# The half-wide chunk of a feed-forward block by seven products: half a slab of the down projection moved ahead of its last block, and the order of ScalarE and VectorE written out by hand

## The chip, the core and the metric

The kernel runs on one core of one Trainium2 chip. The core has TensorE (PE) for matmuls, which reads SBUF and writes PSUM; VectorE (DVE) and ScalarE (ACT) for elementwise work; GpSimd (POOL); and SyncE (SP), which mostly issues transfers. ACT and POOL issue some transfers too. Each engine has its own queue and works through it in order; engines wait for each other by semaphores. The metric is the time of one execution on the device in microseconds (us), and the median of several runs is compared.

## What is computed

Two layers over 256 tokens of width 1024. Each layer has a feed-forward block, a mixer (a gated convolution, a recurrence and a pooling), a cross attention over 256 rows of memory, and a second feed-forward block, each with a residual and a layer norm behind it:

```
def swiglu(x, w_gate, w_up, w_down):
    return (jax.nn.silu(x @ w_gate) * (x @ w_up)) @ w_down

for l in range(DEPTH):
    h = layer_norm(ALPHA * h + 0.5 * swiglu(h, ffn1_gate[l], ffn1_up[l], ffn1_down[l]), ln_g[l, 0], ln_b[l, 0])
    ...
    h = layer_norm(ALPHA * h + mix, ln_g[l, 1], ln_b[l, 1])
    h = layer_norm(ALPHA * h + cross_attn(h, mem, ca_q[l], ca_k[l], ca_v[l], ca_o[l]), ln_g[l, 2], ln_b[l, 2])
    h = layer_norm(ALPHA * h + 0.5 * swiglu(h, ffn2_gate[l], ffn2_up[l], ffn2_down[l]), ln_g[l, 3], ln_b[l, 3])
```

All is float32; the inner width of the feed-forward block is 2816.

## The kernel before

**Halves of a number.** A float32 product is made of three matmuls on rounded parts. `split` (L74) makes the parts: ACT rounds a tile (the cast on L75, `whi` or `ah`), then DVE subtracts the rounded from the whole (L76, `wlo` or `al`, called the rest below). `mm_rows` (L153) multiplies the rounded by the rounded, the rounded by the rest, and the rest by the rounded. Each weight loaded from memory goes through such a split, 1024 columns of 128 partitions at a time.

**Chunks.** A feed-forward block (`ffn`, L420) goes through its inner width in chunks of 512 columns, and a last one of 256, number 5, the half-wide chunk. For each chunk it makes gate and up products, the activation times the up product (called acts), and then multiplies acts by rows of the down matrix into four banks that add up over the block (`both`, L765). Rows of the down matrix come in slabs of two times 128 (`slab`, L741): (3,0) and (3,1) belong to chunk 3, (4,0) and (4,1) to chunk 4, (5,0) to chunk 5. A slab is two splits, an ACT cast and a DVE rest for each.

**By seven products.** Some chunks are made by `by_seven` (L600) with seven products of 2x2 blocks in place of eight: chunks 2 and 4, and chunk 5 in every feed-forward block but the first. `run` (L650) is one block product of 12 matmuls for a bank `o[n]`, `parts_of` (L633) adds two weight blocks on DVE where it is told to (L637) and splits the sum, `taken` (L668) copies a bank to SBUF on ACT (L669), and `put` (L655) adds or subtracts a bank on DVE (L656). In the half-wide chunk the steps of L691 to L696 run in reverse order: first the product for `o[3]`, then the one that adds to `o[0]` and is copied to `f`; then comes the last block, with the weights w00 + w10 added and split for it (L698). Ahead of these, `taken(e, o[0])` (L687) copies the bank that the reversed step writes again.

**Dealing.** The acts have to be turned, so that the inner width lies on the partitions. `turn` (L464) issues four transfers that deal out the gated tile (L469); for the half-wide chunk two are on SP and two on ACT. Its inner function `rest` makes the transposes on DVE (L475) and splits the result into `ah` and `al` (L480). `left` (L700) runs the activation of the second half (L454) and a sum, and `gate_all` (L704) multiplies by the up product (L705) and calls `turn`.

**Order.** The program's text gives priorities; a scheduler puts each engine's instructions in order at build time. `tc.issue_after(x)` ties instructions of the block to come behind `x` on the engine of `x`, and leaves the other engines free. In the half-wide chunk the list `between` names what is put between the blocks: half of slab (3,0) (its `k` = 0), and the dealing of chunk 4's acts. Behind the chunk (L806 to L812) come the transposes and split of chunk 4's acts, tied behind the last rest on DVE; then activation, product and turning of chunk 5's acts in one call; then the other half of slab (3,0) and slab (3,1). Slabs (4,0), (4,1) and (5,0) are loaded on L816 and multiplied in `ending` (L822), for the first 128 tokens and then for the second. `finish` (L323) makes the layer norm of the first 128 tokens while PE works on the second, and PE transposes the result (L196) ahead of its last 12 matmuls of the block where another stage follows.

Of the kernel before, what the change touches and what calls it, by code (L numbers as in the profile page):

```python
# [11 lines left out]
AF = mybir.ActivationFunctionType  # L12
# [48 lines left out]
def model(ctx: ExitStack, tc: tile.TileContext, t: dict, out: bass.AP):  # L61
# [12 lines left out]
    def split(hi, lo, src):  # L74
        nc.scalar.copy(hi, src)  # L75
        lows.append(nc.vector.tensor_tensor(lo, src, hi.bitcast(F32), op=ALU.subtract))  # L76
# [343 lines left out]
    def ffn(l, name, n, pend=None, last=False, early=None):  # L420
        gate, up, down = (t[f"{name}_{x}"][l] for x in ("gate", "up", "down"))
        with tc.tile_pool(name="ffn", bufs=2, reuse_waits="tile") as fp:
# [24 lines left out]
            def ordered(v):  # L447
                return v.rearrange("p (a k j) -> p a k j", a=4, j=32)

            def in_order(o):  # L450
                return o.rearrange("p (a j k) -> p a k j", a=4, j=32)

            def activate(s, i, og):
                nc.scalar.activation(ordered(s[:, i, :]), in_order(og), AF.Silu)  # L454

            def gated(s, i, ou):
                v = ordered(s[:, i, :])
# [6 lines left out]
            def turn(s):  # L464
                n = s.shape[2] // P
                x = fp.tile([P, 4, NT, P], F32, tag="dealt", name="dealt", bufs=1)[:, :, :, 0 : 32 * n]
                for a in range(4):
                    queue = nc.scalar if n < 4 and a % 2 else nc.sync
                    queue.dma_start(x[a * 32 : a * 32 + 32], s[:, :, a * 32 * n : (a + 1) * 32 * n])  # L469

                def rest():
                    ah, al = act_tiles()
                    d = fp.tile([P, NT, 4, P], F32, tag="up", name="square", bufs=1)[:, :, 0:n, :]
                    for i in range(NT):
                        nc.vector.transpose(  # L475
                            d[:, i].rearrange("p k (b r) -> p b k r", b=4),
                            x[:, :, i, :].rearrange("p b (k j) -> p b k j", k=n),
                        )
                    d = d.rearrange("p i k t -> p k i t")
                    split(*(y[:, 0:n].rearrange("p k (i t) -> p k i t", i=NT) for y in (ah, al)), d)  # L480
                    return ah, al

                return rest
# [116 lines left out]
            def by_seven(c0, ncol, bx, between):  # L600
# [54 lines left out]
                def put(o, a, op, b):  # L655
                    nc.vector.tensor_tensor(ordered(o), in_order(a), ordered(b), op=op)  # L656
# [8 lines left out]
                def bank():  # L665
                    return acc((P, CHUNK))[:, 0:ncol]

                def taken(o, bank):  # L668
                    nc.scalar.copy(ordered(o), in_order(bank))  # L669

                def more(to, m, j):
                    for i, x in enumerate(to):
# [11 lines left out]
                run(o[0], bx[1], parts_of(w00, w11), True)  # L684
                if ncol == CHUNK:
                    more(w00, gate, 1)
                taken(e, o[0])  # L687
                between[1]()
                nc.scalar.activation(s[:, 0, :], s[:, 0, :], AF.Silu)
                put(e, o[1], ALU.subtract, e)  # L690
                steps = [  # L691
                    lambda: (run(o[0], bx[2], parts_of(w01), True), taken(f, o[0])),
                    lambda: (o.append(bank()), run(o[3], bx[3], parts_of(w11))),
                ]
                for step in steps if ncol == CHUNK else steps[::-1]:
                    step()  # L696
                put(f, o[1], ALU.subtract, f)
                run(o[0], part_of_x(1, 1), parts_of(w00, None if ncol == CHUNK else w10), True)  # L698

                def left():  # L700
                    activate(s, 1, o[0])
                    put(e, o[3], ALU.add, e)

                    def gate_all():  # L704
                        passed.append(nc.vector.tensor_tensor(s, s, ef, op=ALU.mult))  # L705
                        return turn(s)

                    return gate_all
# [3 lines left out]
            def last_hidden(c0, turn=None):  # L712

                ah, al = act_tiles()
                s = activations()[:, 0, :].rearrange("p (j c) -> p j c", j=2)
                r = fp.tile([P, NT, CHUNK], F32, tag="up", name="up", bufs=1)[:, 0, :].rearrange("p (j c) -> p j c", j=2)
                for m, o in ((gate, s), (up, r)):
                    if turn and m is gate:
                        with tc.issue_after(passed[-1].ins):
# [25 lines left out]


            sevens = (2, 4) if early is not None else (2, 4, 5)
            passed, turn_memory = [], None
            bx = []

            if early is None:
# [23 lines left out]
            for c, (c0, ncol) in enumerate(chunks):  # L775
                if not c:
                    acts.append(first()())
                    ys = [[acc((P, 512), "dn") for _ in range(2)] for _ in range(NT)]
                elif c in sevens:
                    half = []  # L780

                    def deal_last():
                        acts[4] = acts[4]()

                    left = by_seven(
                        c0, ncol, bx,
                        [lambda: both(*todo.pop(0))] * 2 if ncol == CHUNK else
                        [lambda: (half.append(slab(3, 0)), both(3, 0, half[0], (0,))), deal_last],
                    )
                else:  # L790
                    acts.append(hidden(c0)() if ncol == CHUNK else last_hidden(c0, turn_memory))
# [563 lines left out]
```

## Time and profile before

| | |
|---|---|
| median of 3 runs | 1067.07 us (1066.81 to 1068.54) |
| the profiled execution, its own time | 1067.7 us |
| its span, from the first to the last instruction | 1066.0 us |
| granted clock of PE, mean | 0.999 |
| bytes moved | 251.06 MB, mean 236 GB/s |

A row of the order of time reads: start in us from the span's beginning, duration in us, engine, line, operation, the tile written, an arrow, the tiles read, shapes, and xN where N instructions in a row are merged; what stands in brackets is how long the engine sat idle before it, and what ended that. Durations of instructions that follow each other on an engine overlap a little, so the step from one start to the next is what an instruction costs its engine. SPq and ACTq are the sequencers that issue transfers. The three half-wide chunks by seven stand near 495 to 510, 663 to 678 and 1021 to 1036 us of the span; the first is the one quoted.

### The profile page before, as it was taken

Reading aid. Unit: us, or ns where it says so; the run is one execution under the profiler, and the core shown is the slowest. Engines: PE = TensorE matmul, PEld = TensorE weight load, DVE = VectorE, ACT = ScalarE, POOL = GpSimd, SP = SyncE. Lnnn points to the kernel's source line nnn. Section 1 sums busy time; section 2 is a strip of 40 time slices with the busy share of each in tenths; the row PEclk is TensorE's granted clock in tenths of the full one; section 3 lists DMA queues with packets and bytes.
Section 4 is the critical chain, followed back from the end, with each engine's and each line's share of the span. In section 5 each row is a group of like instructions: output and inputs, shape, how many; then the busy total and the mean of one; then the engine's idle time right before and its main releaser. Section 6 shows DMA issues by size and latency. Waiting matters only on the chain.

```text
span 1066.0 us, 16501 instructions
## 1 busy us (share of the span) xinstructions
PE 1053.4 (99%) x6014; PEld 935.8 (88%) x6014; DVE 933.8 (88%) x1246; ACT 661.9 (62%) x909; POOL 90.8 (9%) x122
## 2 busy tenths in 40 slices
PE   9999999999999999999999999999999999999997
PEld 7888888889899888888888888888898998888886
DVE  6998898989988789887998987989899788899887
ACT  6675775677557566655665756666764655675661
POOL 8001001000000001010001001010000000000000
PEclk9999999999999999999999999999999999999999
DMA  9999984754675589978788987866636665799862
GB/s 364 293 317 274 259 276 151 256 169 157 207 277 178 165 282 237 357 188 223 246 295 229 332 248 204 273 221 221 200 119 220 241 236 172 239 291 305 242 188 68
DMA packets 143745, 251.06 MB, mean 236 GB/s; under 512 B 12784, under 2 KB 53520, under 8 KB 143664
## 3 DMA queue, kind: packets, MB, share of 16 engines
q1 hardware_dynamic: 130656, 228.89, 64.4%
q0 software_dynamic: 10800, 19.55, 10.7%
q10 hardware_dynamic: 2208, 1.57, 0.5%
q8 instruction: 47, 0.77, 0.3%
q14 instruction: 34, 0.28, 0.1%
HBM read 234.50 MB, written 1.05 MB: 221 GB/s over the span
## 4 chain that ended last, share of the span: by engine, by line
PE 93%; DVE 4%; issue 1%; ACT 1%; DMA 1%; DVEq 0%; ACTq 0%
PE acc L129 61%; PE dn L129 29%; DVE wlo L76 2%; PE acc L196 1%; DVE raw L637 1%; ACT whi L75 1%; PE dn L1040 0%; DMA lng<-in_ln_g_dram 0%; DMA h<-in_x_dram 0%; PE dn L1114 0%; PE acc L517 0%; DVE halves L656 0%; PE dn L1113 0%; PE dn L1102 0%; PE acc L1182 0%
## 5 line engine op out<-in xcount | busy, mean ns | idle before, releaser
L75 ACT CAST whi<-raw 128x1024 fp32r<-128x1024 f32 (+1 forms) x453 | 457.1, 1042 | 207.8 <-PE dn L129 62.8
L76 DVE TENSOR_TENSOR wlo<-raw,whi 128x1024 fp32r<-128x1024 f32 (+1 forms) x453 | 534.8, 1210 | 54.6 <-ACT whi L75 49.9
L129 PE MATMUL acc<-whi,xT 128*128 128x512 f32 (+1 forms) x1064 | 314.1, 373 | 0.0
L129 PEld LDWEIGHTS acc<-whi,xT 128*128 128x128 f32 x1064 | 199.1, 189 | 27.5 <-ACT both L669 0.9
L129 PE MATMUL acc<-wlo,xT 128*128 128x512 f32 (+1 forms) x532 | 197.9, 372 | 0.0
L129 PE MATMUL dn<-whi,ah 128*128 128x512 f32 x346 | 131.5, 380 | 0.0
L129 PE MATMUL dn<-wlo,ah 128*128 128x512 f32 x346 | 131.1, 379 | 0.0
L129 PE MATMUL dn<-whi,al 128*128 128x512 f32 x346 | 130.8, 379 | 0.0
L129 PE MATMUL acc<-xT,whi 128*128 128x512 f32 x480 | 117.8, 382 | 0.2
L129 PEld LDWEIGHTS acc<-wlo,xT 128*128 128x128 f32 x532 | 100.6, 189 | 13.2
L129 PEld LDWEIGHTS acc<-xT,whi 128*128 128x128 f32 x480 | 86.6, 190 | 10.5 <-ACT whi L75 0.7
L129 PE MATMUL dn<-whi,xT 128*128 128x512 f32 x288 | 87.7, 380 | 0.0
L129 PEld LDWEIGHTS dn<-whi,al 128*128 128x128 f32 x346 | 65.4, 189 | 9.3
L129 PEld LDWEIGHTS dn<-whi,ah 128*128 128x128 f32 x346 | 65.4, 189 | 9.0
L129 PEld LDWEIGHTS dn<-wlo,ah 128*128 128x128 f32 x346 | 65.4, 189 | 8.9
L129 PEld LDWEIGHTS acc<-xT,wlo 128*128 128x128 f32 x480 | 62.9, 191 | 3.2
L129 PE MATMUL acc<-whi,kTh 128*128 128x512 f32 (+1 forms) x176 | 62.0, 352 | 3.2 <-ACT both L669 3.2
L129 PE MATMUL acc<-xT,wlo 128*128 128x256 f32 x480 | 63.2, 275 | 0.0
L129 PE MATMUL acc<-wlo,kTh 128*128 128x512 f32 (+1 forms) x176 | 61.7, 351 | 0.0
L129 PE MATMUL acc<-whi,kTl 128*128 128x512 f32 (+1 forms) x176 | 61.7, 351 | 0.0
L129 PEld LDWEIGHTS dn<-whi,xT 128*128 128x128 f32 x288 | 54.4, 189 | 7.4
L129 PE MATMUL dn<-wlo,xT 128*128 128x512 f32 x144 | 54.6, 379 | 0.0
(245 smaller groups left out, 1291.2 us busy)
## 6 DMA issues: line engine op xcount, KB each, us to landing
raw<-in_ffn_up_dram SPq DMA_DIRECT2D x88, 512.0 KB, 5.4
raw<-in_ffn_down_dram SPq DMA_DIRECT2D x88, 512.0 KB, 5.7
raw<-in_ffn_gate_dram SPq DMA_DIRECT2D x84, 512.0 KB, 5.6
raw<-in_w_in_dram SPq DMA_DIRECT2D x48, 512.0 KB, 4.5
dealt<-sg SPq DMA_DIRECT2D x80, 128.0 KB, 4.8
raw<-in_ffn_up_dram POOLq DMA_DIRECT2D x19, 512.0 KB, 6.1
raw<-in_ffn_gate_dram POOLq DMA_DIRECT2D x16, 512.0 KB, 9.9
raw<-in_ca_k_dram SPq DMA_DIRECT2D x16, 512.0 KB, 5.2
```

Of the source, the lines that this page charges most:

```text
L75: nc.scalar.copy(hi, src)
L76: lows.append(nc.vector.tensor_tensor(lo, src, hi.bitcast(F32), op=ALU.subtract))
L129: nc.tensor.matmul(o, w, x, start=start, stop=stop, skip_group_check=more)
L196: turns.append(nc.tensor.transpose(pt[:, k, :], src[:, (4 * j + k) * P : (4 * j + k + 1) * P], unit))
L637: nc.vector.tensor_tensor(r[i], r[i], plus[i], op=ALU.add)
```

## The change

In the half-wide chunk, and behind it:

- the cast for w00 + w10 is tied behind the copy of L687 on ACT;
- the second half of slab (3,0) moves from behind the chunk to between the copy to `f` and the last block;
- the split of chunk 4's acts (not its transposes) is held back, until the activation of L454 has been issued on ACT and the product of L705 on DVE;
- the transposes and the split of chunk 5's acts move from ahead of slab (3,1) to behind the loads of (4,0) and (4,1);
- the splits of (4,0), (4,1) and (5,0) and of chunk 5's acts are tied behind the last transfer that deals chunk 5's acts (that one is issued on ACT, so the tie holds the casts) and behind the product of L705 (so it holds the rests); the last two also behind the last rest of (4,1).

Chunks of 512 columns keep their order; `activate` and `taken` only return their instruction.

```diff
@@ turn
-                    queue.dma_start(x[a * 32 : a * 32 + 32], s[:, :, a * 32 * n : (a + 1) * 32 * n])
-
-                def rest():
+                    last_deal = queue.dma_start(x[a * 32 : a * 32 + 32], s[:, :, a * 32 * n : (a + 1) * 32 * n])
+
+                deals.append(last_deal)
+
+                def rest(behind=None):
...
-                    split(*(y[:, 0:n].rearrange("p k (i t) -> p k i t", i=NT) for y in (ah, al)), d)
+
+                    def parts():
+                        split(*(y[:, 0:n].rearrange("p k (i t) -> p k i t", i=NT) for y in (ah, al)), d)
+
+                    if behind is None:
+                        parts()
+                    else:
+                        behind.append(parts)
                     return ah, al
@@ by_seven
-                taken(e, o[0])
+                copied = taken(e, o[0])
                 between[1]()
                 nc.scalar.activation(s[:, 0, :], s[:, 0, :], AF.Silu)
                 put(e, o[1], ALU.subtract, e)
-                steps = [
-                    lambda: (run(o[0], bx[2], parts_of(w01), True), taken(f, o[0])),
-                    lambda: (o.append(bank()), run(o[3], bx[3], parts_of(w11))),
-                ]
-                for step in steps if ncol == CHUNK else steps[::-1]:
-                    step()
-                put(f, o[1], ALU.subtract, f)
-                run(o[0], part_of_x(1, 1), parts_of(w00, None if ncol == CHUNK else w10), True)
+                if ncol == CHUNK:
...
+                else:
+                    o.append(bank())
+                    run(o[3], bx[3], parts_of(w11))
+                    run(o[0], bx[2], parts_of(w01), True)
+                    taken(f, o[0])
+                    put(f, o[1], ALU.subtract, f)
+                    with tc.issue_after(copied.ins):
+                        w = parts_of(w00, w10)
+                    between[2]()
+                    run(o[0], part_of_x(1, 1), w, True)
 
                 def left():
-                    activate(s, 1, o[0])
+                    act = activate(s, 1, o[0])
                     put(e, o[3], ALU.add, e)
 
                     def gate_all():
-                        passed.append(nc.vector.tensor_tensor(s, s, ef, op=ALU.mult))
+                        passed.append((act, nc.vector.tensor_tensor(s, s, ef, op=ALU.mult)))
                         return turn(s)
@@ ffn
-                        [lambda: (half.append(slab(3, 0)), both(3, 0, half[0], (0,))), deal_last],
+                        [lambda: (half.append(slab(3, 0)), both(3, 0, half[0], (0,))), deal_last, lambda: both(3, 0, half[0], (1,))],
...
                     if ncol < CHUNK:
+                        held = []
                         with tc.issue_after(lows[-1].ins):
-                            acts[4] = acts[4]()
-                    acts.append(left() if c + 1 in sevens else left()()())
+                            acts[4] = acts[4](held)
+                    acts.append(left() if c + 1 in sevens else left()() if c == 5 else left()()())
                     if ncol < CHUNK:
-                        both(3, 0, half[0], (1,))
+                        with tc.issue_after(passed[-1][0].ins), tc.issue_after(passed[-1][1].ins):
+                            held[0]()
                         both(3, 1)
...
-            end = [slab(4, 0), slab(4, 1), slab(5, 0)]
+            with ExitStack() as behind:
+                if 5 in sevens:
+                    behind.enter_context(tc.issue_after(deals[-1].ins))
+                    behind.enter_context(tc.issue_after(passed[-1][1].ins))
+                end = [slab(4, 0), slab(4, 1)]
+                if 5 in sevens:
+                    behind.enter_context(tc.issue_after(lows[-1].ins))
+                    acts[5] = acts[5]()
+                end.append(slab(5, 0))
```

More of the change, by code (lines that the diff above doesn't have):

```diff
@@ L453, in activate @@
             def activate(s, i, og):
-                nc.scalar.activation(ordered(s[:, i, :]), in_order(og), AF.Silu)
+                return nc.scalar.activation(ordered(s[:, i, :]), in_order(og), AF.Silu)
             def gated(s, i, ou):
@@ L668, in taken @@
                 def taken(o, bank):
-                    nc.scalar.copy(ordered(o), in_order(bank))
+                    return nc.scalar.copy(ordered(o), in_order(bank))
                 def more(to, m, j):
@@ L690, in by_seven @@
                 put(e, o[1], ALU.subtract, e)
[L691 to L698 removed]
+                if ncol == CHUNK:
[4 more added lines that the diff above has]
+                    put(f, o[1], ALU.subtract, f)
+                    run(o[0], part_of_x(1, 1), parts_of(w00), True)
+                else:
+                    o.append(bank())
+                    run(o[3], bx[3], parts_of(w11))
+                    run(o[0], bx[2], parts_of(w01), True)
+                    taken(f, o[0])
+                    put(f, o[1], ALU.subtract, f)
+                    with tc.issue_after(copied.ins):
+                        w = parts_of(w00, w10)
+                    between[2]()
+                    run(o[0], part_of_x(1, 1), w, True)
                 def left():
[L701 removed]
+                    act = activate(s, 1, o[0])
                     put(e, o[3], ALU.add, e)
                     def gate_all():
[L705 removed]
+                        passed.append((act, nc.vector.tensor_tensor(s, s, ef, op=ALU.mult)))
                         return turn(s)
@@ L718, in last_hidden @@
                     if turn and m is gate:
-                        with tc.issue_after(passed[-1].ins):
+                        with tc.issue_after(passed[-1][1].ins):
                             turn(0, 0)
@@ L747, in ffn @@
             sevens = (2, 4) if early is not None else (2, 4, 5)
-            passed, turn_memory = [], None
+            passed, deals, turn_memory = [], [], None
             bx = []
```

## The prediction

> **What bounds the kernel now.** I read the page first, then who waited for whom on TensorE (PE), then the order of time on PE, ScalarE (ACT) and VectorE (DVE) around the half-wide chunk.
>
> ```profile
> PE 1053.4 (99%) x6014; PEld 935.8 (88%) x6014; DVE 933.8 (88%) x1246; ACT 661.9 (62%) x909; POOL 90.8 (9%) x122
> PE 93%; DVE 4%; issue 1%; ACT 1%; DMA 1%; DVEq 0%; ACTq 0%
> PE acc L129 <- ACT both L669: 3.2, 3, 1.1
> ```
>
> The first row is busy time, the second the chain that ended last, the third the one wait of PE that is not at the kernel's start: three times, 1.1 us each, PE waits for the copy on L669. That is the half-wide chunk, once in each of the three feed-forward stages that have it by seven products. PE is busy 1053.4 of 1066.0 us, so no more than some 12 us of gaps can be won anywhere, and here no more than what the next fence shows. It is PE in the first of the three stages (start, duration, what):
>
> ```profile
> 504.91 0.28 PE L129 MATMUL acc<-wlo,kTh 128*128 128x256 f32 x1
> 505.02 0.28 PE L129 MATMUL acc<-whi,kTl 128*128 128x256 f32 x1
> 506.42 0.38 PE L129 MATMUL acc<-whi,kTh 128*128 128x256 f32 x1 [1.13 <-ACT both L669]
> 506.64 0.28 PE L129 MATMUL acc<-wlo,kTh 128*128 128x256 f32 x1
> ...
> 508.08 0.38 PE L129 MATMUL dn<-wlo,ah 128*128 128x512 f32 x1
> 508.30 0.38 PE L129 MATMUL dn<-whi,al 128*128 128x512 f32 x1
> 508.59 0.38 PE L129 MATMUL acc<-whi,xT 128*128 128x256 f32 x1
> ...
> 510.03 0.38 PE L129 MATMUL dn<-whi,ah 128*128 128x512 f32 x1
> ```
>
> A 256-column matmul follows the one before it by 0.11 us (504.91 to 505.02), a 512-column one by 0.216 (508.08 to 508.30). So the gap at 505.02 costs 1.40 - 0.11 = 1.29, the slow step behind it 0.22 - 0.11 = 0.11, the step at 508.30 0.29 - 0.22 = 0.07: **1.47 us in a stage, 4.4 in three**. That is all that the change can win on PE here. Now ACT and DVE:
>
> ```profile
> 505.06 1.04 ACT L75 CAST whi<-raw 128x1024 fp32r<-128x1024 f32 x1 [2.88 <-DVE raw L637]
> 506.01 0.37 ACT L669 COPY both<-acc 128x256 f32<-128x256 f32 x1
> 506.27 1.99 ACT L75 CAST whi<-raw 128x1024 fp32r<-128x1024 f32 x2
> 508.16 0.37 ACT L669 COPY both<-acc 128x256 f32<-128x256 f32 x1
> 508.43 2.00 ACT L75 CAST whi<-raw 128x1024 fp32r<-128x1024 f32 x2
> 510.40 1.04 ACT L75 CAST ah<-square 128x1024 fp32r<-128x1024 f32 x1
> 511.35 0.38 ACT L454 ACTIVATE both<-acc 128x256 f32<-128x256 f32 x1
> 511.63 1.98 ACT L75 CAST whi<-raw 128x1024 fp32r<-128x1024 f32 x2
> 513.58 1.55 ACTq L469 DMA_DIRECT2D dealt<-both  x2
> 515.17 1.99 ACT L75 CAST whi<-raw 128x1024 fp32r<-128x1024 f32 x2 [1.56 <-DVE wlo L76]
> ```
>
> ```profile
> 503.75 1.22 DVE L637 TENSOR_TENSOR raw<-raw 128x1024 f32<-128x1024 f32 x1
> 506.13 1.23 DVE L76 TENSOR_TENSOR wlo<-raw,whi 128x1024 fp32r<-128x1024 f32 x1 [1.17 <-ACT whi L75]
> 507.27 0.42 DVE L656 TENSOR_TENSOR both<-acc,both 128x256 f32<-128x256 f32 x1
> 507.61 1.22 DVE L76 TENSOR_TENSOR wlo<-raw,whi 128x1024 fp32r<-128x1024 f32 x1
> ...
> 509.08 1.29 DVE L475 STREAM_TRANSPOSE square<-dealt 128x512 f32<-128x512 f32 x2
> ...
> 511.73 1.22 DVE L76 TENSOR_TENSOR al<-square,ah 128x1024 fp32r<-128x1024 f32 x1
> 512.86 0.69 DVE L705 TENSOR_TENSOR both<-both 128x512 f32<-128x512 f32 x1
> 513.46 6.90 DVE L76 TENSOR_TENSOR wlo<-raw,whi 128x1024 fp32r<-128x1024 f32 x6
> 520.27 0.77 DVE L475 STREAM_TRANSPOSE square<-dealt 128x256 f32<-128x256 f32 x2
> 520.96 1.18 DVE L76 TENSOR_TENSOR wlo<-raw,whi 128x1024 fp32r<-128x1024 f32 x1
> 522.07 0.68 DVE L76 TENSOR_TENSOR al<-square,ah 128x512 fp32r<-128x512 f32 x1
> ```
>
> ```profile
> 510.00:525.00 15.00, 15.00 (x72) 13.15 (x72) 14.60 (x18) 8.22 (x10) 0.00 (x0) 1.00 0.88 283
> ```
>
> The cause of the gap is plain: at 505.06 ACT casts the last weights (w00 + w10), having stood 2.88 us for their addition on DVE (503.75), and the copy that PE waits for stands behind that cast until 506.01. The last row counts busy time in the 15 us behind it: PE 15.00, no gap, but DVE 14.60, nearly as full. From 506.13 on, DVE hardly stops. So PE and DVE bind together here, and a change that brings PE forward has to bring DVE's chain forward too.
>
> **The change part by part** (times of this first stage).
>
> *The copy ahead of the cast.* The block that fills the copied bank is the 12 matmuls before the 12 that end with 505.02, so its last starts at 505.02 - 12 x 0.111 = 503.69. The second copy started at 508.16, 0.41 behind the last matmul of its block (506.64 + 10 x 0.111 = 507.75); so the first can start at 504.10 and is done at 504.47, before PE's next block wants it at 505.13. The cast stays at 505.06, since its addition ends at 504.97. Gain: 1.29 + 0.11. DVE may also do the subtraction of 507.27 in its idle 1.17 us before 506.13, which frees 0.33 (507.27 to 507.61).
>
> *Half a slab ahead of the last block.* No work is added; 12 matmuls of 512 columns move. PE: block of 12 from 505.13 to 506.47 (12 x 0.111), half slab to 509.06 (12 x 0.216), last block to 510.40. Its second copy could start at 506.36 + 0.41 = 506.77; should two casts go first it still ends by 508.3; the weights' rests are ready at 507.36. Both are hidden behind the half slab, and the 0.07 goes. Without that cover the block would wait for the copy. But the last block now ends at 510.40, where its last matmul stands about 0.4 us later than today's.
>
> *Activation before the cast to ah.* Today the activation waits behind the cast of 510.40 and starts at 511.35. Now it starts at 510.29 + 0.41 = 510.70 and ends at 511.08. DVE's product on L705 needs DVE as well: from 506.13 it has two rests at 1.135 (six rests take 520.27 - 513.46 = 6.81), a subtraction 0.33, two transposes 1.25, another sum 0.33 and the second rest of slab (3,1) 1.135, until 511.46. The product then ends at 512.15 instead of 513.55. The rest al moves behind it; it is wanted only after slab (3,1), so it costs nothing if something else is slower.
>
> *Slabs (4,0), (4,1) behind the dealing.* This is the part that costs. Today the casts of (4,0) stand at 508.43 and those of (4,1) at 511.63, both ahead of the two transfers that ACT issues at 513.58. The change ties them, and so everything that DVE does with them, behind these. The transfers wait for the product (512.15) and take ACT 1.55 us: to 513.73. First cast to 514.78, its rest from 514.82 to 516.04. DVE has only al to do between 512.06 and that point (to 513.28) and stands idle for some 1.6 us. PE comes from the last block with 24 matmuls of slab (3,1), 510.40 + 5.18 = 515.58, and wants that rest with its second matmul, 515.79: 0.3 late. The second rest comes 1.135 later, where PE has 0.65 of work between: 0.5 late. The two of (4,1) come in time, since each half there serves 12 matmuls, 2.6 us. Then transposes (0.69 from start to start, 520.27 to 520.96), a rest 1.135, al 0.60, a rest 1.135 from 519.36: the last starts at 521.79 and ends at 523.0, some 0.65 behind PE's need. **Given back: 0.3 + 0.5 + 0.65 = 1.45.** Nothing in the queues of SP or POOL is moved past these; SP issues loads as buffers come free, so those of the next stage's weights start 1.3 us later (they wait for the first rest of (4,0), 514.68 today, 516.04 then).
>
> [...] Were issuing free for ACT, the casts would start at 512.2, the rests could follow al without a gap, and the stage would keep nearly all of its 1.45.
>
> *Acts of the last chunk behind the rests of (4,1).* The transposes stand today at 520.27 and would stand at 519.36. Their data land in time:
>
> ```profile
> DMA to landing us min/median/max: 2.3/2.8/3.4
> 525.13 0.69 DVE L352 SCALAR_TENSOR_TENSOR h<-h,dn 128x512 f32<-128x512 f32 x1 [0.17 <-PE dn L129]
> 530.11 1.04 PE L196 MATMUL acc<-pdn,h 128*128 128x128 f32 x8
> ```
>
> Issued by 513.0, landed by 516.4 at the slowest. The other two rows are the normalization of the first half: 5.0 us from its last sum to its transposes on PE, with PE full until then. This leaves no slack, so if next-stage rests (one at 520.96 today) come between, PE waits for what they cost. That is bounded from below by nothing and from above by one rest, 1.135, in two of the stages (behind the last one there is no next). I take 0: the rests come later with their loads, and a higher-priority sum goes first.
>
> **The sum.** 1.47 off, 1.45 back in each stage, three stages: 0.0 on the profiled execution, whose span is 1066.0 and whose own time is 1067.7; the median of the runs is 1067.07, 0.6 below. Forecast **1067.1 us**. Unknowns: DVE's order. If the product goes ahead of the second rest of (3,1), the chain starts 0.35 sooner: -0.4 a stage. If a next-stage rest comes ahead of the last ones, +1.1 in each of two stages. So the likeliest case's own range is 1065.6 to 1069.2.
>
> **Rivals.** *The whole stall goes and nothing takes its place.* PE could be given other matmuls at the late rests: those with the cast half alone (c. 1 us earlier than the rest), or the second half of the tokens. For it: the casts come 1.26 us ahead of the rests (505.06, then 506.13 + 1.23), and PE's order is not fixed by hand there. Against it: DVE's chain to 523.0 stays, and the normalization follows it. It gives 2.2 to 4.4 less: 1062.7 to 1064.9, middle 1063.8.
>
> *Slower: DVE's idle time before the held rests decides.* From the point where ACT's casts wait for the transfers, DVE loses 1.6 us; the same rests, plus the next stage's, then stand ahead of the first half's normalization, and PE waits at the transposes of 530.11. Price, in the two stages that have a next one: one rest, 1.135, ahead of the last slab, and a second, half hidden, 0.57, at the transposes: 3.4 in all, 1070.5; from 2.3 (the first alone, 1069.4) to 4.5 (both whole, 1071.6). It decides from the moment when one next-stage rest is put ahead of the last slab's. For it: at 520.96 one stands there today. Against it: its load starts 1.3 us later.
>
> *The change does not do what it says*: the copy is issued first but PE still waits, as its bank is not free. Against: nothing else stands in front of that copy. It would be 0.0 for the copy and some 1.4 us a stage for the held slabs, 1071; I give it 2 in 100, within the slower case.
>
> **How the numbers follow.** Forecast 0.46, full gain 0.25, slower 0.29. About 0.2% (2.1 us) is what a measurement of this kernel tells from no change. Nearly all of the full gain lies beyond it; of the likeliest case about 0.01 each way. Faster 0.25, same 0.46, slower 0.29. The range leaves out the far quarter of the gain (0.06) and the far third of the slower case (0.10): 1063.2 to 1070.9.
>
> **What would show it.** Right: PE's wait for L669 is gone; the activation starts near 510.7 and the product ends near 512.2 on this clock; ACT has no cast of a slab between it and its two transfers; DVE idles 1 to 2 us before the first rest of (4,0); and PE shows new gaps of 0.3 to 0.7 us at slabs (4,0) and (5,0), adding up to some 1.4. Wrong: no gap there (gain), or a gap of a microsecond at the transposes (loss).

## The result, and the profile after

| | median (us) | runs | over before |
|---|---|---|---|
| before | 1067.12 | 8, 1066.67 to 1068.61 | |
| after | 1069.83 | 8, 1069.39 to 1073.36 | 1.0029 [1.0017, 1.0042] |

The change made the kernel slower: by 2.7 us by the medians, and by a ratio of 1.0029 whose interval is clear of 1. That is inside the range, on the side of the slower rival; the likeliest case, no change, did not come true.

The profiled execution of the kernel after took 1073.36 us, the longest of its eight, so stages are compared here more than spans. In this execution the first half-wide chunk stands some 0.5 us later than before, PE having waited longer for its input at the start (1.1 us, and 0.6 before): the last block, forecast from 509.06, starts at 509.58. That is the shift of 0.52 below. In the code after, L678 is the copy of L669, L723 the product of L705, L477 the transposes of L475; L352 is the sum that ends a half of the down projection, and L362, L366, L373, L378 are the four steps of its normalization on DVE.

First the busy time on the page:

```profile
PE 1055.8 (99%) x6014; PEld 936.4 (87%) x6014; DVE 933.4 (87%) x1246; ACT 662.8 (62%) x909; POOL 91.2 (9%) x122
```

Then who waited for whom on PE (in total, times, longest):

```profile
PE acc L196 <- DVE h L378: 3.7, 2, 1.9
PE dn L129 <- DVE wlo L76: 1.3, 2, 1.0
```

The wait for the copy (3.2 us in three stages) is gone. In its place stand two waits of 1.9 us at the transposes of the normalized first half, and one of 1.0 for a rest. The two rows sum to 5.0, 1.8 more than the row that went.

The spans of the two profiled executions lie further apart, 1066.0 and 1071.4 us. PE's rows divide the 5.4 us. The half-wide chunk of the first stage starts 0.5 later. From its first row to the transposes PE takes 1.0 longer (495.95 to 530.11 before, 496.47 to 531.63 after), and 0.8 longer in the second stage (664.06 to 698.16, 665.83 to 700.70). Between the stages 2.4 are lost, an estimated 1.8 of it to the lower clock of the last section. The third stage takes 0.1 longer up to the last matmul, and 0.6 more pass behind that (7.34 and 7.96 us to the end); the cause of these 0.6 was not looked for.

PE in the first stage, in order of time:

```profile
506.99 0.38 PE L129 MATMUL dn<-whi,ah 128*128 128x512 f32 x1
...
509.36 0.38 PE L129 MATMUL dn<-whi,al 128*128 128x512 f32 x1
509.58 0.27 PE L129 MATMUL acc<-whi,xT 128*128 128x256 f32 x1
...
516.12 1.03 PE L129 MATMUL dn<-whi,ah 128*128 128x512 f32 x4
...
521.75 0.38 PE L129 MATMUL dn<-wlo,ah 128*128 128x512 f32 x1
522.25 0.48 PE L129 MATMUL dn<-whi,ah 128*128 128x512 f32 x1
...
529.40 0.38 PE L129 MATMUL dn<-whi,al 128*128 128x512 f32 x1
531.63 1.29 PE L196 MATMUL acc<-pdn,h 128*128 128x128 f32 x8 [1.85 <-DVE h L378]
```

Half slab and last block run without a gap. At 516 PE runs four products with the rounded acts and weights in a row, where it would have waited for a rest. At slab (5,0) one step of 0.50 is left, and then no gap of that size until the transposes, a step of 2.23. Why their data are late stands in ACT's and DVE's order:

```profile
504.51 0.37 ACT L678 COPY both<-acc 128x256 f32<-128x256 f32 x1 [1.51 <-PE acc L129]
505.87 2.94 ACT L75 CAST whi<-raw 128x1024 fp32r<-128x1024 f32 x3 [0.99 <-DVE raw L646]
508.71 0.36 ACT L678 COPY both<-acc 128x256 f32<-128x256 f32 x1
511.12 0.38 ACT L454 ACTIVATE both<-acc 128x256 f32<-128x256 f32 x1 [2.04 <-PE acc L129]
...
512.92 1.57 ACTq L469 DMA_DIRECT2D dealt<-both  x2
514.54 5.78 ACT L75 CAST whi<-raw 128x1024 fp32r<-128x1024 f32 x6 [2.10 <-DVE al L76]
```

```profile
512.21 0.68 DVE L723 TENSOR_TENSOR both<-both 128x512 f32<-128x512 f32 x1
512.81 1.22 DVE L76 TENSOR_TENSOR al<-square,ah 128x1024 fp32r<-128x1024 f32 x1
515.62 4.63 DVE L76 TENSOR_TENSOR wlo<-raw,whi 128x1024 fp32r<-128x1024 f32 x4 [1.59 <-ACT whi L75]
520.17 0.77 DVE L477 STREAM_TRANSPOSE square<-dealt 128x256 f32<-128x256 f32 x2
...
522.23 0.69 DVE L76 TENSOR_TENSOR al<-square,ah 128x512 fp32r<-128x512 f32 x1 [0.19 <-ACT ah L75]
522.84 2.35 DVE L76 TENSOR_TENSOR wlo<-raw,whi 128x1024 fp32r<-128x1024 f32 x2
525.11 0.68 DVE L352 SCALAR_TENSOR_TENSOR h<-h,dn 128x512 f32<-128x512 f32 x1
...
525.71 0.69 DVE L352 SCALAR_TENSOR_TENSOR h<-h,dn 128x512 f32<-128x512 f32 x1
...
526.32 1.22 DVE L76 TENSOR_TENSOR wlo<-raw,whi 128x1024 fp32r<-128x1024 f32 x1
527.46 0.21 DVE L362 TENSOR_SCALAR mv<-st 128x1 f32<-128x1 f32 x1
528.74 0.69 DVE L352 SCALAR_TENSOR_TENSOR h<-h,dn 128x512 f32<-128x512 f32 x1 [1.06 <-PE dn L129]
...
529.35 0.15 DVE L366 TENSOR_SCALAR rs<-mv 128x1 f32<-128x1 f32 x1
```

Behind its activation ACT rounds ah, and then makes no cast until 514.54: it waits for the product and issues the two transfers. DVE idles 1.59 and 0.19 us. Eight rests of weights (and two of acts, `al`) follow the product before the mean (L362) is made: six of the slabs and two of the next stage. The first of these two ends the pair of 522.84; the second, at 526.32, has fallen into the normalization, between the two sums and the mean. Behind the mean the second half's sum (528.74) stands ahead of `rs`, so that `rs` comes 1.89 us behind the mean. In the kernel before it came 1.52 behind, with nothing between:

```profile
525.86 0.21 DVE L362 TENSOR_SCALAR mv<-st 128x1 f32<-128x1 f32 x1
527.38 0.15 DVE L366 TENSOR_SCALAR rs<-mv 128x1 f32<-128x1 f32 x1 [1.31 <-ACT kTh L365]
```

On the clock of the kernel before, the second sum stands at 525.19 (525.71 less 0.52), where it stood at 525.13, and the mean at 526.94, where it stood at 525.86. So up to the sums DVE is no later than before; it only fails to follow PE's lead. What makes this stage slower than before comes behind the sums: a rest that before stood ahead of them, and the sum ahead of `rs`.

In the third stage, which no next one follows, another step is displaced: a sum on L339 that waits for PE stands ahead of the held rests, on DVE, and PE then waits for the first of these:

```profile
1046.53 0.69 DVE L339 SCALAR_TENSOR_TENSOR h<-h,dn 128x512 f32<-128x512 f32 x1 [2.60 <-PE dn L129]
1047.13 3.49 DVE L76 TENSOR_TENSOR wlo<-raw,whi 128x1024 fp32r<-128x1024 f32 x3
```

### The profile page after: what moved, and what is told of

Read it like the earlier page. It is cut to its first block, busy times and chain, and to the rows that moved or that the text cites. A ratio compares the mean times of both kernels' runs of the same rounds, so it can differ in the third digit from the quotient of the medians.

```text
span 1071.4 us, 16492 instructions
## 1 busy us (share of the span) xinstructions
PE 1055.8 (99%) x6014; PEld 936.4 (87%) x6014; DVE 933.4 (87%) x1246; ACT 662.8 (62%) x909; POOL 91.2 (9%) x122
## 3 DMA queue, kind: packets, MB, share of 16 engines
q10 hardware_dynamic: 2208, 1.57, 0.5%
## 4 chain that ended last, share of the span: by engine, by line
PE 86%; DVE 5%; issue 3%; DMA 3%; ACT 1%; POOL 0%; ACTq 0%; DVEq 0%; SPq 0%; POOLq 0%
PE acc L129 58%; PE dn L129 25%; DVE wlo L76 2%; DMA raw<-in_ffn_gate_dram 2%; PE acc L196 1%; ACT whi L75 1%; DVE raw L646 1%; DMA raw<-in_w_out_dram 0%; PE dn L1068 0%; DMA h<-in_x_dram 0%; PE dn L1142 0%; PE acc L526 0%; DMA dealt<-both 0%; DVE h L378 0%; DVE yr L1221 0%
```

## The experiments

All times are medians, each with its ratio to runs of the kernel before on the same chip, and its interval. "Idle" is DVE's idle time in the first stage from the product to the mean, without the waits for PE; "L196" is PE's wait at the transposes, in total.

| kernel | us | ratio | idle | L196 |
|---|---|---|---|---|
| after | 1069.83 | 1.0029 [1.0017, 1.0042] | 1.78 | 3.7 |
| copy_first | 1065.90 | 0.9987 [0.9978, 0.9996] | 0 | 0 |
| half_back | 1071.09 | 1.0037 [1.0024, 1.0050] | 1.61 | 3.3 |
| slabs_free | 1064.15 | 0.9972 [0.9962, 0.9982] | 0 | 0 |
| casts_free | 1063.38 | 0.9966 [0.9953, 0.9978] | 0 | 0 |
| split_early | 1072.61 | 1.0054 [1.0041, 1.0068] | 2.98 | 3.7 |
| next_later | 1068.62 | 1.0015 [1.0006, 1.0024] | 1.66 | 2.2 |
| free_next | 1064.81 | 0.9977 [0.9968, 0.9986] | 0 | 0.5 |
| flips_first | 1064.35 | 0.9974 [0.9965, 0.9982] | 0 | 0 |
| behind_act | 1072.51 | 1.0040 [1.0026, 1.0054] | 1.80 | 3.7 |
| casts_flips | 1064.93 | 0.9973 [0.9963, 0.9984] | 0.40 | 0 |
| sp_deal | 1067.68 | 1.0006 [0.9997, 1.0015] | 0.94 | 3.3 |
| sp_next | 1066.59 | 0.9993 [0.9984, 1.0002] | 0.69 | 2.3 |

### The copy alone (copy_first)

```diff
@@ the kernel before
-                taken(e, o[0])
+                copied = taken(e, o[0])
...
-                run(o[0], part_of_x(1, 1), parts_of(w00, None if ncol == CHUNK else w10), True)
+                with nullcontext() if ncol == CHUNK else tc.issue_after(copied.ins):
+                    w = parts_of(w00, None if ncol == CHUNK else w10)
+                run(o[0], part_of_x(1, 1), w, True)
```

> The kernel before with one edit of the change: the cast of w00 + w10 tied behind the copy on ACT. If PE alone binds behind the half-wide chunk, all of its stall goes, 1.4 us in each of three stages: about 1063. If DVE's chain binds there with it, as the working of the prediction has it, only what DVE wins goes on to the end (one subtraction, 0.33 us, done in its idle time): 0.3 to 0.6 us a stage, about 1065.8, and the transposes of the first half's normalization wait for DVE. If the copy itself were the cause of the slower time, this would be slower than before.

By the medians it is 1.2 us faster than before. That is the time that the expectation gives for DVE's chain, but not by its mechanism: the transposes do not wait for DVE at all (L196 is 0). The copy's own wait is gone, and the next copy's takes its place, at the last block. Who waited:

```profile
PE acc L129 <- ACT both L669: 2.2, 3, 0.8
```

And PE at that place:

```profile
507.07 0.38 PE L129 MATMUL dn<-whi,ah 128*128 128x512 f32 x1
508.19 0.38 PE L129 MATMUL acc<-whi,xT 128*128 128x256 f32 x1 [0.74 <-ACT both L669]
```

So of 3.2 us waited, 2.2 come back one block later, which is what the half slab is there to cover.

### The half slab put back (half_back)

```diff
@@ the kernel after
-                        [lambda: (half.append(slab(3, 0)), both(3, 0, half[0], (0,))), deal_last, lambda: both(3, 0, half[0], (1,))],
+                        [lambda: (half.append(slab(3, 0)), both(3, 0, half[0], (0,))), deal_last],
...
-                    between[2]()
...
                             held[0]()
+                        both(3, 0, half[0], (1,))
                         both(3, 1)
```

> The changed kernel with the second half of slab (3,0) put back behind the chunk; everything else stays. If the later last block (its last matmul 0.4 us later, and all the chain of activation, product and dealing behind it) is the loss, some 0.5 to 1 us a stage comes back: 1067 to 1068. If the held slabs are the loss, the chain only starts somewhat sooner and PE meets a new short wait at the last block: within 0.7 of the changed kernel, 1069 to 1070.

The wait at the last block is back, as in the experiment before:

```profile
PE acc L196 <- DVE h L378: 3.3, 2, 1.6
PE acc L129 <- ACT both L678: 2.2, 3, 0.7
```

PE waits 0.7 in each stage there, and 0.2 less at each transposes. The time, 1071.09, lies above both ranges of the expectation and 1.3 us above after's, but the two intervals overlap. So the later last block is not the loss; that the half slab hides the copy is shown by the row, and its worth in this kernel is not fixed.

### The held slabs let go (slabs_free, casts_free)

```diff
@@ slabs_free
-                if 5 in sevens:
-                    behind.enter_context(tc.issue_after(deals[-1].ins))
-                    behind.enter_context(tc.issue_after(passed[-1][1].ins))
                 end = [slab(4, 0), slab(4, 1)]
+                if 5 in sevens:
+                    behind.enter_context(tc.issue_after(deals[-1].ins))
+                    behind.enter_context(tc.issue_after(passed[-1][1].ins))
```

In casts_free only the first of the two ties, that behind the transfer, is moved.

> The changed kernel without one tie: slabs (4,0) and (4,1) are not held behind the dealing and the product (acts of chunk 5 and slab (5,0) still are). If the 1.6 us that DVE idles behind the held casts are the loss, the idle time goes, the transposes no longer wait 1.9 us for the normalization in the first two stages and the gap of 1.3 us in the third stage goes: 1065 to 1066.5, faster than before. If the moved half slab is the loss, it stays near 1069.5.

> The changed kernel with the casts of slabs (4,0) and (4,1) no longer behind the dealing on ACT; their rests stay behind the product on DVE. If the loss is the time that ACT stands in the transfers (product, 1.55 us of issuing, then the first cast), it is gone and the time is within 0.7 of the version with the slabs wholly free, 1064.2: 1063.5 to 1065. If the rests held on DVE carry it, it stays above 1068.

These are the two best versions; both came out somewhat faster than was expected of them (casts_free by 0.1 us). casts_free differs from the kernel after in one tie, that of the casts of (4,0) and (4,1) behind ACT's second transfer, and that is worth 6.4 us: 1069.83 to 1063.38. ACT and DVE in its first stage:

```profile
507.62 2.96 ACT L75 CAST whi<-raw 128x1024 fp32r<-128x1024 f32 x3
510.49 0.37 ACT L454 ACTIVATE both<-acc 128x256 f32<-128x256 f32 x1
```

```profile
510.89 0.69 DVE L723 TENSOR_TENSOR both<-both 128x512 f32<-128x512 f32 x1
511.50 1.22 DVE L76 TENSOR_TENSOR wlo<-raw,whi 128x1024 fp32r<-128x1024 f32 x1
...
524.34 0.21 DVE L362 TENSOR_SCALAR mv<-st 128x1 f32<-128x1 f32 x1
525.86 0.15 DVE L366 TENSOR_SCALAR rs<-mv 128x1 f32<-128x1 f32 x1 [1.31 <-ACT kTh L365]
```

Three casts are done while ACT waits for the last block (it stood idle 2.04 us there in the kernel after), a rest is ready at once behind the product, and `rs` follows the mean by 1.52 again. From the activation to the mean it is 13.85 us (510.49 to 524.34) against 16.34 (511.12 to 527.46). Of the 2.49, 1.78 is DVE's idle time and 0.69 the product, which comes 1.09 behind the activation and not 0.40.

### More idle time (split_early)

```diff
@@ the kernel after
-                            acts[4] = acts[4](held)
+                            acts[4] = acts[4]()
...
-                        with tc.issue_after(passed[-1][0].ins), tc.issue_after(passed[-1][1].ins):
-                            held[0]()
```

> The changed kernel with the split of chunk 4's acts as before, not held behind the activation and the product. DVE then has nothing at all between the product and the held rests, but product, transfers and casts stand 1 us later, as the cast to ah is ahead of the activation again. If the chain from the last block to the held casts sets the time, this is slower than the changed kernel by 0.3 to 0.9 in each stage: 1070.5 to 1072.5. If holding that split is itself harmful, it is faster than 1069.5.

Here the rest al of chunk 4 goes ahead of the product, and DVE has nothing left for the time of the transfers: it idles 2.98 us and not 1.78, and the time is 2.8 us above after's. The two intervals just touch (1.0042 and 1.0041), so that holding that split back helps is likely and not more.

### The next stage's rests moved (next_later, free_next)

Both tie the splits of the next stage's first weights behind the mean of the first half on DVE; next_later in the kernel after, free_next in slabs_free.

```diff
+                if i == 0:
+                    means.append(mean)
...
-                wg = load(gate, 0, NK, 0, CHUNK, fine=pend is None)
-                wu = load(up, 0, NK, 0, CHUNK) if pend is not None else None
+                with tc.issue_after(means[-1].ins) if l and name == "ffn1" else nullcontext():
+                    wg = load(gate, 0, NK, 0, CHUNK, fine=pend is None)
+                    wu = load(up, 0, NK, 0, CHUNK) if pend is not None else None
...
-        w = load(t["ca_k"][l], 0, NK, c * CHUNK, CHUNK, across=True)
+        with tc.issue_after(means[-1].ins) if l and not c else nullcontext():
+            w = load(t["ca_k"][l], 0, NK, c * CHUNK, CHUNK, across=True)
```

> The changed kernel with the rests of the next stage's weights tied behind the mean of the first half's normalization on DVE, in the two stages that have a next one. If the rests of the next stage that stand ahead of and inside that normalization (1.135 us each) carry the wait at the transposes, most of 2 x 1.9 us goes: 1066.5 to 1067.5, and only the third stage's gap is left. If DVE's idle time behind the held slabs alone carries it, the wait shrinks by less than half: 1068.5 to 1069.5.

> The version with the slabs free, and the rests of the next stage tied behind the mean of the first half's normalization as well. With the slabs free PE no longer waits at the transposes (no such wait in its trace), so if that wait was the only way in which the next stage's rests cost, nothing is left to win: 1063.7 to 1064.7. If they also keep DVE from the acts of the last chunk (PE waits 0.63 us there), up to 1 us more: 1063.2.

next_later is 1.2 us below after by the medians, with intervals that overlap, and the wait shrinks from 3.7 to 2.2; these are the figures that the expectation has for idle time alone, but the rows show a tie that missed its aim. free_next wins nothing of slabs_free, and lies 0.1 above its range. DVE in next_later, where `rs` is on L368:

```profile
525.11 0.22 DVE L362 TENSOR_SCALAR mv<-st 128x1 f32<-128x1 f32 x1
525.24 2.35 DVE L76 TENSOR_TENSOR wlo<-raw,whi 128x1024 fp32r<-128x1024 f32 x2
527.50 0.15 DVE L368 TENSOR_SCALAR rs<-mv 128x1 f32<-128x1 f32 x1
```

The tie only moved the rests to the other side of the mean: two of them stand ahead of `rs` now, which comes 2.39 behind the mean. So these runs do not show what the kernel would take with none there. An estimate from the rows: without the two, `rs` would come 2.39 - 1.52 = 0.87 sooner, and of the 1.1 us that PE waits at each transposes some 0.2 would be left.

### A hold without the issuing (behind_act, sp_deal, sp_next)

```diff
@@ behind_act
-                    behind.enter_context(tc.issue_after(deals[-1].ins))
+                    behind.enter_context(tc.issue_after(passed[-1][0].ins))
...
                 end = [slab(4, 0), slab(4, 1)]
+                if 5 in sevens:
+                    behind.enter_context(tc.issue_after(deals[-1].ins))
@@ sp_deal
-                    queue = nc.scalar if n < 4 and a % 2 else nc.sync
+                    queue = nc.sync
```

sp_deal has the first edit too, and for (5,0) as well; sp_next is sp_deal with the tie of next_later.

> The kernel after with the casts of slabs (4,0) and (4,1) tied behind the activation of L454 on ScalarE instead of behind the second dealing transfer; their rests stay tied behind the product on VectorE, the casts of (5,0) behind the transfer. Theory A (the 1.55 us in which ScalarE issues its two transfers, and the wait for the product ahead of them, hold the casts and leave VectorE idle, and that is the whole loss): the first held cast starts near 511.1 on the clock of the kernel before and not near 513.7, its rest can follow the product near 512.2, VectorE idles less than 0.3 us there, and the time is 1063.3 to 1064.8. Theory B (any tie that puts these casts behind the chunk costs, since three casts fewer are done ahead of the activation than in the version without a tie): ScalarE becomes late by about one cast, 0.95 us a stage, and the time is 1065.5 to 1068.

> The kernel after with all four dealing transfers of chunk 5's acts on SP instead of two on ScalarE, and the casts of slabs (4,0), (4,1) and (5,0) tied behind the activation of L454 on ScalarE; the rests stay tied behind the product on VectorE. So the casts still stand behind the chunk, but nothing on ScalarE waits for the product or issues a transfer ahead of them. (With the transfers left on ScalarE and the casts tied behind the activation, the scheduler put the transfers ahead of them again, and the time was that of the kernel after.) Theory A (waiting for the product and 1.55 us of issuing hold the casts, and that is the whole loss): the first held cast starts near 510.9 to 511.2, VectorE idles under 0.5 us, the waits of 1.9 us at the transposes L196 shrink below 0.5, and the time is 1063.2 to 1064.8. Theory B (any tie that puts these casts behind the chunk costs): VectorE still idles about 1 us a stage, and the time is 1065.5 to 1068.

> The version with all four dealing transfers on SP and the casts tied behind the activation (1067.7 us: VectorE does not idle ahead of the held rests, but rests of the next stage's weights stand ahead of the normalization and in it, and TensorE waits 1.6 us at the transposes in two stages), and with the splits of the next stage's first weights tied behind the first half's mean on VectorE. Theory A (VectorE's idle time and those rests ahead of the transposes are together the whole loss against the version with free casts, 1063.4 us; each alone won 1.2 to 2.2 us): the waits at L196 shrink below 0.6 each and the time is 1063.4 to 1065.2. Theory B (the hold behind the activation itself costs, whatever stands ahead of the normalization): 1065.8 to 1067.5.

behind_act told nothing of its question: a tie behind the activation leaves the transfers free to go first, the build put them first, and the idle time (1.80) and the waits (3.7) are those of the kernel after. In sp_deal the transfers are off ACT:

```profile
510.58 1.04 ACT L75 CAST ah<-square 128x1024 fp32r<-128x1024 f32 x1
511.52 5.77 ACT L75 CAST whi<-raw 128x1024 fp32r<-128x1024 f32 x6
520.40 0.62 ACT L75 CAST ah<-square 128x512 fp32r<-128x512 f32 x1 [3.11 <-DVE square L477]
```

The casts follow without a gap, the idle time ahead of the first held rest is gone, and 2.1 us are won. Theory A misses: 0.68 us of idle time come later on DVE, for the cast to ah on chunk 5 (520.40), and 0.26 for a cast of the next stage; a rest still stands in the normalization, and PE still waits 1.6 us at each transposes. Theory B's figures come true (0.94 us of idle time, 1067.68), but its reason, that any such tie costs, does not hold in the third stage. There DVE idles 0.69 us too, and later still has to wait for PE:

```profile
1048.69 0.69 DVE L76 TENSOR_TENSOR al<-square,ah 128x512 fp32r<-128x512 f32 x1 [0.69 <-ACT ah L75]
1050.60 0.69 DVE L352 SCALAR_TENSOR_TENSOR h<-h,dn 128x512 f32<-128x512 f32 x1 [1.22 <-PE dn L129]
```

From the first row of the half-wide chunk to the last matmul PE takes 35.7 us in that stage (1022.68 to 1058.41), in casts_free 35.6 (1019.57 to 1055.16), and in the kernel after 36.7. In the first stage sp_deal needs 1.6 us more than casts_free to the transposes (495.65 to 530.03, 495.48 to 528.30). So a hold behind the activation costs next to nothing where no next-stage rests follow and DVE has time to spare; its loss is in the two stages where they do follow.

sp_next comes out at 1066.59, outside theory A and inside B; its waits at the transposes are 1.1 us each, behind the two rests that the tie puts ahead of `rs`. So waiting for the product and issuing is about 2.1 of the 6.4 us. A version with the hold behind the activation and every next-stage rest behind the normalization was not tried.

### What is left to win (flips_first, casts_flips)

flips_first is slabs_free, and casts_flips casts_free, with the rests of (5,0) tied behind the transposes of chunk 5's acts:

```diff
...
                     acts[5] = acts[5]()
+                    behind.enter_context(tc.issue_after(flips[-1].ins))
```

> The version with the slabs free, and the first rest of slab (5,0) tied behind the transposes of chunk 5's acts on DVE (it stood ahead of them). The wait that is left on PE there is for al, 0.63 + 0.10 us in two stages and some 1.2 in the third. If DVE's order is what makes al late, al comes up to 1.1 us sooner and the waits go: 1061.8 to 1063. If the two rests behind it become the next wait, it stays near 1064.2.

> The version with the casts of (4,0) and (4,1) free (1063.4 us), and slab (5,0)'s rests tied behind the transposes of chunk 5's acts, so that these and the rest al come first. Theory A (TensorE's three gaps of 0.3 to 0.5 us for al are all that is left, and VectorE has room for the order): 1062.2 to 1063.0. Theory B (VectorE is full until the normalization, and what is put first there pushes a rest into the place ahead of the normalization, as was seen with both ties of slabs 4 taken away): within 0.4 us of 1063.4.

Neither gains. In flips_first the waits for al, 0.9 us in three, are gone, and no time is won (1064.35 against 1064.15). In casts_flips the transposes stand 0.40 us for their data instead; it is 1.5 us above casts_free by the medians, outside both theories, though the two intervals overlap.

```profile
517.47 0.78 DVE L477 STREAM_TRANSPOSE square<-dealt 128x256 f32<-128x256 f32 x2 [0.40 <-DMA dealt<-both]
```

## Why the prediction was right in its parts and wrong in the sum

**Right: the copy.** Less the shift it starts at 503.99 (forecast 504.10), and PE does not wait for it. copy_first shows it alone.

**Right: the half slab.** No gap at the last block, and the last block ends where it was put: its last matmul at 510.81, or 510.29 without the shift of 0.52, against 510.29 (510.40 - 0.11). Without it PE waits 0.7 (half_back).

**Right: ACT and DVE up to the held rests.** Less the shift, the activation starts at 510.60 (forecast 510.70), the product ends at 512.37 (512.15), the first held cast starts at 514.02 (513.73), and DVE idles 1.59 us (some 1.6). The forecast had the casts wait for the 1.55 us in which ACT issues its two transfers, and the trace agrees: the cast of 514.54 begins 0.05 behind the end of 512.92 + 1.57, and in the three stages of both kernels the next cast begins 0.03 to 0.05 behind the end of the issuing. With these transfers on SP (sp_deal) it begins right behind the cast to ah (511.52, where the cast to ah starts at 510.58 and takes 1.04).

**Wrong without cost: "landed by 516.4 at the slowest".** The transfers that deal these acts took 3.8 to 5.3 us from issue to landing in the kernel after, and not 2.3 to 3.4. Counted from the same 513.0, the slowest land at 518.3, still ahead of the transposes, which stand at 519.65 less the shift. In casts_flips the transposes come sooner and wait for their data.

**Wrong: "Given back: 0.3 + 0.5 + 0.65 = 1.45", at slabs (4,0) and (5,0).** This is the step that failed, with its other half, "I take 0" for the next stage's rests. PE did not wait at (4,0) at all: its order was built with other matmuls there, four with the cast half in a row, which the gain rival had named. At (5,0) it lost 0.28 (521.75 to 522.25, less 0.216). But what PE does in another order changes nothing in DVE's chain. DVE had the same eight rests to make ahead of the mean as in casts_free, and 1.78 us less to make them in. The delay was paid not where the first late rest was wanted, but at the next point where PE needs the end of DVE's chain and has no other matmul to run: the transposes. There it costs 1.85 us of waiting in each of two stages, and 1.0 for a displaced sum in the third. The "0" for the next stage's rests measured 1.08 us at the mean and 0.37 more at `rs`, against the kernel before. That the time lies in the range is owed to the slower rival, which the range took in, and not to this sum.

**The slower rival** had the place and nearly the size: next-stage rests ahead of the first half's normalization, waits at the transposes, 1.7 us a stage, 1069.4 to 1071.6; the gap of a microsecond at the transposes, named as what would show a loss, is there. Its mechanism was only in part what happened. Its point of decision, a next-stage rest ahead of the last slab's, was not needed: one next-stage rest stands behind the last slab's, one fell in behind the sums (526.32), and the second half's sum ahead of `rs` added 0.37 (1.89 - 1.52); neither that sum nor the third stage was in it.

**The gain rival** was right that PE is not bound to wait at the late rests, and wrong that the gain follows. Its 1062.7 to 1064.9 is what slabs_free and casts_free reach, where no tie holds the casts.

What is shown: one tie on ACT makes the difference between 0.34% faster and 0.29% slower by the ratios, and DVE is never idle between product and mean in the three fastest versions. How the 6.4 us divide between the idle time, the rest inside the normalization and the sum ahead of `rs` is only bounded: each was moved, but none could be taken away alone. The third stage of sp_deal shows that idle time alone, with room behind it, cost next to nothing there (0.69 us of it; 35.7 us against 35.6 in casts_free).

## What to carry to other kernels

Behind the half-wide chunk PE and DVE were both full (15.00 and 14.60 of 15 us before the change). There the idle time that the change brought on DVE, 1.78 us, was paid at the next point where PE needs the end of DVE's chain (1.85 us of waiting at the transposes), not where the first late piece is used; where a second engine is as full, follow its chain to such a point before summing. In the third stage of sp_deal, where DVE had time to spare before that point, 0.69 us of idle time cost next to nothing (35.7 us against 35.6 in casts_free). The tie behind a transfer that ACT issues held all tied work for the transfer's own wait and its issuing too (2.10 us without a cast, 1.57 of them the issuing): tie to what must come first, and leave free the work that could fill the engine's wait. Look at the order that the build makes around a new gap: here it filled one with work that then stood in the way of something urgent (in the third stage the sum of 1046.53, ahead of the held rests).

## What was not expected of the hardware

PE's clock fell behind one of the two long gaps. In the kernel after, the 512-column matmuls follow each other by 0.43 us behind the gap of the second stage, twice the 0.216 of elsewhere:

```profile
700.70 1.29 PE L196 MATMUL acc<-idn,h 128*128 128x128 f32 x8 [1.85 <-DVE h L378]
701.75 0.67 PE L129 MATMUL dn<-whi,ah 128*128 128x512 f32 x1
702.21 0.63 PE L129 MATMUL dn<-wlo,ah 128*128 128x512 f32 x1
702.64 0.64 PE L129 MATMUL dn<-whi,al 128*128 128x512 f32 x1
...
705.46 0.38 PE L129 MATMUL dn<-whi,ah 128*128 128x512 f32 x1
```

The busy time by stretches has the granted clock behind the five engines:

```profile
532.00:537.00 5.00, 4.96 (x27) 4.25 (x26) 5.00 (x8) 4.53 (x6) 0.00 (x0) 1.00 0.52 157
701.00:706.00 5.00, 4.97 (x20) 3.96 (x18) 3.69 (x5) 3.56 (x5) 0.00 (x0) 0.66 0.41 113
```

It was 0.66 behind the second gap and 1.00 behind the first, though both are steps of 2.23 us. From 701.75 to 705.46 it is 3.71 us where nine steps at 0.216 are 1.94: about 1.8 us lost. The same showed in split_early behind its first gap (0.66 from 532 to 537), and behind neither gap of behind_act's profiled run (1.00). The executions of behind_act fall into two groups: 1069.3 and 1069.5, with a mean granted clock of 0.998, and 1072.5 to 1073.0, with 0.995. In the kernel after, 1070.8, 1072.1 and 1073.4 have 0.995 or 0.996, and the other five, up to 1070.1, have 0.998. A mean that is lower by 0.003 over 1070 us is an estimated 3.2 us, about what lies between the groups. So the clock goes with the long executions; that it fell behind these gaps in each of them is likely and was not shown. The length of a gap alone does not decide it; what does was not shown.
